# An fp32 decoder trunk on one core: one plain block instead of two at the start of three channel mixers

## The chip, the cores and the metric

The kernel runs on one core of a Trainium2 chip, as one launch. Its time is the device time of an execution in microseconds, given as the median of several runs. A core has five engines with queues of their own: PE (matrix products, with the weight loads shown apart as PEld), DVE (vector work), ACT (activations and copies), POOL (general work) and SP, which here only issues transfers (DMAs). SBUF is the memory that the engines work from, PSUM holds the matrix products in eight banks, and DRAM is outside the core.

## The reference

A trunk of two layers works on `x` of 512 tokens by 1024 channels in float32, and ends in an RMSNorm. Each layer has two channel mixers around a token mixer: latent attention (MLA) in layer 0, sparse attention (NSA) in layer 1.

```python
def rmsnorm(x, g):
    y = x * lax.rsqrt(jnp.mean(x * x, axis=-1, keepdims=True) + RMS_EPS)
    return y * g

def swiglu(x, w_gate, w_up, w_down):
    return (jax.nn.silu(x @ w_gate) * (x @ w_up)) @ w_down

for i in range(2):
    h = h + 0.5 * swiglu(rmsnorm(h, ffn_norm_a[i]), ffn_a_w_gate[i], ffn_a_w_up[i], ffn_a_w_down[i])
    h = h + mixer_i(rmsnorm(h, mix_norm[i]))        # MLA, then NSA
    h = h + 0.5 * swiglu(rmsnorm(h, ffn_norm_b[i]), ffn_b_w_gate[i], ffn_b_w_up[i], ffn_b_w_down[i])
return rmsnorm(h, final_norm)
```

The change touches the channel mixers alone. There are four of them, called a0, b0, a1 and b1 in order of time, with `idx` 0 to 3. `w_gate` and `w_up` are 1024 x 2816, `w_down` is 2816 x 1024.

## The kernel before

**Layout.** The residual is kept transposed: eight tiles `h` (channels c, 128 partitions, 512 tokens in the free dimension). A product of weights and activations is made in three matrix products, since each operand is split into a rounded high part and the remainder: high by high, high by low, low by high. A split (`split`, L173 to L181) is one ACT copy that rounds (L177) and one DVE subtraction that leaves the low part (L178). The norm's gain is a factor in the split of `h`; the factor 1/rms of a token is one row of 512 numbers, which is multiplied in behind the matrix products.

**A channel mixer** (`ffn`, L416) runs over 22 hidden blocks of 128 hidden columns, f = 0 to 21. A block yields the gate and the up projection, each 128 hidden columns by 512 tokens, in one of two forms:

- A *plain* block (`plain`, L404): for the gate and the up slab, 8 channel chunks, 2 halves of the tokens and 3 products, 96 matmuls of 128x256.
- A *sums* block (`wsums`, L328, and `product`, L371): the 2 x 2 product of (gate, up weights, by halves of the channels) and (activations, by halves of channels and tokens) in seven products instead of eight, each of 4 chunks x 3, 84 matmuls of 128x256. The seven products are run in the order 1, 7, 6, 2, 5, 4, 3 (L532 to L545). Products 1, 2 and 3 use raw quarters of the activations; products 7, 6, 5 and 4 use sums of quarters. Of the weights, products 1 and 2 use the gate slab's halves, 4 the second half of the up slab, and 7, 6, 3 and 5 use sums of halves, which DVE adds (L359, L360, L363, L364) and ACT and DVE split.

`PLAIN = 3, 2, 2, 2` (L50) is the number of plain blocks at the start of each mixer. While these run, the sums of the activations are made (`combine`, L231, once for each pair p = 0 to 3 of chunks p and p + 4): ACT scales two `h` tiles into `y` (L240), DVE makes four quarters' sums in `u` (L244 to L246), and ACT and DVE split `u` into a tile `four` (L177, L178). Tiles `y` and `u` are taken from the rotating tags `fh` and `fl`, three buffers each, which also hold the split weights of the sums blocks.

**The plain blocks' weights** of mixers 1 to 3 are not split there. They are finished during the mixer before: at its blocks 12 to 20 `make_load` fetches a quarter slab, `make` splits it, and POOL writes the high and the low half to DRAM (L396); at the mixer's start `made_slab` (L398) loads 1 MiB, both parts of a slab, into one of three weight tiles (L401).

**The norm's row** of mixers 1 to 3 comes out of the first plain block's squares: PE sums them over partitions (L269), POOL takes the power, DVE transposes (L292), and POOL sends the result through DRAM, spread to all partitions (L293, L295, tile `row<-nrow`). The gates of the plain blocks (`gate`, L425: DVE times the row, ACT's Silu, DVE times the row) wait for it.

**From the sums blocks on** a block's matrix products end in ACT's copies: product 1 from bank `px` to `pg` (L533), 7 and 6 to the tile `uq` (L535, L537; one buffer), 5 to `pg` (L540). Two DVE additions finish the up half (L542, L544). Behind each block stand pieces of the down projection (`unit`, L460), the products of 128x512 of L169 to L171, from the third or so block on.

**What sets the order.** Every engine works its queue in order. The queue's order follows the program, with what is ready earlier by the scheduler's model ahead of what is late; `high_priority` puts a few instructions ahead, and `issue_after` puts instructions behind a given one on their engine. So the weight instructions of the second sums block stand behind the copies of the first (`after(copies, i)` in `wsums`, L357 to L368).

Of the kernel before, what the change touches and what calls it, by code (L numbers as in the profile page):

```python
# [49 lines left out]
PLAIN = 3, 2, 2, 2  # L50
# [3 lines left out]
READY = 12  # L54
# [11 lines left out]
class Kern:  # L66
# [13 lines left out]
    def setup(self):  # L80
# [4 lines left out]
        self.nw, self.odd, self.nq, self.made, self.quarter = 0, 0, 0, {}, {}  # L85
# [145 lines left out]
    def combine(self, p):  # L231


        nc, fp = self.nc, self.fp
        y = fp.tile([P, 1024], F32, tag="fh", bufs=3, name="y")
        u = fp.tile([P, 1024 + 2 * PAD], F32, tag="fl", bufs=3, name="u")[:, :1024]
        for e in range(2):
            c = p + KP * e
            with self.tc.issue_after(self.weights.ins) if self.weights else nullcontext():
                nc.scalar.activation(y[:, e * S : e * S + S], self.h[c], AF.Copy, scale=self.gains[:, self.ng + c : self.ng + c + 1])  # L240
            self.weights = None
        q = lambda t, i: t[:, i * HS : i * HS + HS]
        two = lambda t: t.rearrange("p (a n) -> p a n", n=HS)
        nc.vector.tensor_tensor(two(u[:, :S]), q(y, 1)[:, None, :].to_broadcast([P, 2, HS]), two(y)[:, 0:4:3, :], op=ALU.subtract)  # L244
# [19 lines left out]
    def norm_col(self, n, s2, urgent=0, eps=None, col=None):  # L264

        nc = self.nc
        pc = self.bank("o", "pc")
# [60 lines left out]
    def wsums(self, idx, f, copies=None):  # L328


        nc, fp, w_gu = self.nc, self.fp, self.a["w_gu"]
        rg = fp.tile([P, 1024], F32, tag="fr", bufs=3, name="rg")
# [27 lines left out]
        nc.vector.tensor_tensor(u0, u0, g0, op=ALU.add)  # L360
# [10 lines left out]
    def product(self, j, w, out, first, last):  # L371
        mm = self.nc.tensor.matmul
        wh, wl = w[j]
        for p in range(KP):
# [5 lines left out]
    def made_tile(self, idx, f, z):  # L380
        if (idx, f, z) not in self.made:
            self.made[idx, f, z] = self.dp.tile([P, 2048], F32, name=f"made{idx}{f}{z}")[:, :]
        return self.made[idx, f, z]

    def make_load(self, idx, i):
        self.raw = self.sp.tile([P, S], F32, tag="s2", bufs=2, name="wm")
        with self.tc.issue_after(self.gate_load.ins):
            self.nc.sync.dma_start(self.raw, self.a["w_gu"][idx, i // 4, i // 2 % 2][:, i % 2 * S : i % 2 * S + S])

    def make(self, idx, i):  # L390

        hi, lo = [self.quarter[2 * (i % 2) + x] for x in range(2)]
        self.split(self.raw, hi, lo)
        d = self.made_tile(idx, i // 4, i // 2 % 2).rearrange("p (z e n) -> p z e n", z=2, e=2)
        for z, t in enumerate((hi, lo)):
            self.nc.gpsimd.dma_start(d[:, z, i % 2, :], f32v(t))  # L396

    def made_slab(self, idx, f, z):  # L398
        wh, wl = self.wtiles("half")
        both = bass.AP(tensor=wh.tensor, offset=wh.offset, ap=[list(wh.ap[0]), [wl.offset - wh.offset, 2], [1, 1024]])  # L400
        self.nc.sync.dma_start(f32v(both), self.made[idx, f, z].rearrange("p (z n) -> p z n", z=2))  # L401
        return [t.rearrange("p (k c) -> p k c", c=P) for t in (wh, wl)]

    def plain(self, idx, f, z, out):  # L404

        wh, wl = self.ahead.pop(0) if self.ahead else self.made_slab(idx, f, z) if idx else self.wslab(self.a["w_gu"][idx, f, z], (KC, P), "half")
# [9 lines left out]
    def ffn(self, idx, gain_next, ap, tp):  # L416
# [8 lines left out]
        def gate(f, g):  # L425

            t = tg[f] = tp.tile([P, S], F32, tag="tg", bufs=2, name="tg")
            nc.vector.tensor_tensor(t, g, row, op=ALU.mult)
# [58 lines left out]
        def plain_acts():  # L487
            for e, g in enumerate(gates):
                gate(e, g)
# [4 lines left out]
        for f, g in enumerate(gates):  # L494
            u = tu[f] = self.bank(("mm", "S")[f % 2], "pu")
            self.plain(idx, f, 0, g)
            if f == 0 and idx:
# [3 lines left out]
                self.norm_col(D, self.s2, URGENT, col=row[:, 0:P:32])  # L501
# [12 lines left out]
            for p in (((0, 1), (2, 3)) if plain == 2 else ((0, 1), (2,), (3,)))[f]:  # L514
                self.combine(p)

        tail, left = (NF - 2) // NG * NG, 1
        for f in range(plain, NF):
# [6 lines left out]
            w = self.wsums(idx, f, copies if idx and f == plain + 1 else None)  # L525
            if f == plain:
# [7 lines left out]
            self.product(7, w, q, True, False)  # L534
# [3 lines left out]
            self.product(2, w, g[:, :HS], False, True)  # L538
# [7 lines left out]
            if f == plain and idx:  # L546
                with self.after(copies, 3):
# [944 lines left out]
```

## Time and profile before

| What | us |
| --- | --- |
| Median of 3 runs | 1856.54 (1856.47 to 1857.44) |
| The profiled execution, its own time | 1855.04 |
| Its span (first to last instruction) | 1853.3 |
| Busy in the span: PE, DVE, ACT, POOL | 1834.6, 1529.1, 1090.8, 275.9 |
| First matmul of a0, b0, a1, b1 | 5.9, 543.2, 877.7, 1507.2 |

The granted clock of PE is full throughout, and the transfers average 117 GB/s. The profile is of one execution, so its durations and its span belong together, and a sum is made against the span; the execution's own time is 1.7 us above it, and the median is 1.5 us above that. A matmul's duration in the trace overlaps the next one's, so its pace is read from starts. MLA lies between the mixers a0 and b0, NSA between a1 and b1; a1 follows b0 directly.

### The profile page before, as it was taken

What the parts mean: (1) busy time and instruction counts of PE and PEld (TensorE: products, weight loads), DVE (VectorE), ACT (ScalarE), POOL (GpSimd) and SP (SyncE); (2) the same over time, 40 slices, a digit from 0 to 9 for tenths busy, and PEclk for the clock granted to TensorE, in tenths of its full rate; (3) what the DMA queues carried; (4) which work ended last, traced back from release to release, by engine and by line L of the source; (5) the groups of instructions that cost most, each with busy time, mean ns of one, the idle gap of its engine ahead of it and who ended that gap; (6) DMA issues with size and microseconds to landing.
All of it is one profiled execution on the core that took longest, in us unless ns stands there. A gap on an engine that the chain in (4) does not pass through costs nothing.

```text
span 1853.3 us, 32953 instructions
## 1 busy us (share of the span) xinstructions
PE 1834.6 (99%) x12392; PEld 1674.9 (90%) x12392; DVE 1529.1 (83%) x2785; ACT 1090.8 (59%) x2033; POOL 275.9 (15%) x398
## 2 busy tenths in 40 slices
PE   8999999999999999999999999999999999999998
PEld 8999999888889999998999999988888889999997
DVE  7988886578779888876998888755988979888885
ACT  7555554579766555544655555426977856555554
POOL 0000000156510000000000000015665500000000
PEclk9999999999999999999999999999999999999999
DMA  7334433142352345433333443233222143333321
GB/s 259 118 120 154 154 124 105 56 110 72 95 176 99 105 143 166 160 115 122 110 115 130 161 160 99 91 106 108 75 86 74 47 163 121 108 107 103 103 90 57
DMA packets 88047, 216.31 MB, mean 117 GB/s; under 512 B 11176, under 2 KB 39232, under 8 KB 87888
## 3 DMA queue, kind: packets, MB, share of 16 engines
q1 hardware_dynamic: 80272, 195.01, 33.2%
q0 software_dynamic: 4512, 14.17, 2.0%
q10 hardware_dynamic: 3104, 5.03, 0.8%
q8 instruction: 97, 1.59, 0.4%
q14 instruction: 62, 0.51, 0.1%
HBM read 192.33 MB, written 14.76 MB: 112 GB/s over the span
## 4 chain that ended last, share of the span: by engine, by line
PE 87%; DVE 7%; ACT 2%; issue 1%; DMA 1%; POOL 1%; SPq 0%; DVEq 0%; ACTq 0%; POOLq 0%
PE pd L169 8%; PE pd L171 8%; PE pd L170 8%; PE px L376 5%; PE px L377 5%; PE px L378 5%; PE pg L376 4%; PE pg L378 4%; PE pg L377 4%; PE pq L376 4%; PE pq L377 4%; PE pq L378 4%; PE o L1295 2%; PE pt L1270 2%; PE po L169 2%; PE po L171 2%
## 5 line engine op out<-in xcount | busy, mean ns | idle before, releaser
L170 PE MATMUL pd<-al,wd 128*128 128x512 f32 x576 | 224.1, 389 | 0.0
L171 PE MATMUL pd<-ah,wd 128*128 128x512 f32 x576 | 224.0, 389 | 0.0
L169 PE MATMUL pd<-ah,wd 128*128 128x512 f32 x576 | 224.0, 389 | 0.0
L376 PE MATMUL px<-four,wh 128*128 128x256 f32 x632 | 175.3, 277 | 2.8 <-ACT uq L537 1.4
L178 DVE TENSOR_TENSOR w<-rg,w 128x1024 fp32r<-128x1024 f32 x79 | 96.3, 1222 | 96.4 <-ACT w L177 96.4
L376 PE MATMUL pq<-four,wh 128*128 128x256 f32 x632 | 174.5, 276 | 0.4 <-DVE tu L439 0.4
L378 PE MATMUL px<-four,wl 128*128 128x256 f32 x632 | 174.7, 276 | 0.0
L377 PE MATMUL px<-four,wh 128*128 128x256 f32 x632 | 174.5, 276 | 0.0
L377 PE MATMUL pq<-four,wh 128*128 128x256 f32 x632 | 174.5, 276 | 0.0
L378 PE MATMUL pq<-four,wl 128*128 128x256 f32 x632 | 174.5, 276 | 0.0
L458 DVE SCALAR_TENSOR_TENSOR h<-pd,h 128x512 f32<-128x512 f32 x216 | 147.0, 681 | 6.1 <-PE pd L171 6.1
L177 ACT ACTIVATE wd<-wdr 128x384 fp32r<-128x384 f32 x192 | 98.5, 515 | 67.9 <-PE pd L170 38.3
L171 PEld LDWEIGHTS pd<-ah,wd 128*128 128x128 f32 x576 | 108.2, 188 | 22.5
L169 PEld LDWEIGHTS pd<-ah,wd 128*128 128x128 f32 x576 | 108.1, 188 | 19.3
L170 PEld LDWEIGHTS pd<-al,wd 128*128 128x128 f32 x576 | 108.1, 188 | 19.4
L376 PEld LDWEIGHTS px<-four,wh 128*128 128x128 f32 x632 | 118.6, 188 | 4.1 <-ACT uq L537 2.1
L177 ACT ACTIVATE w<-rg 128x1024 fp32r<-128x1024 f32 x79 | 83.8, 1060 | 61.9 <-PE pg L378 56.6
L376 PEld LDWEIGHTS pq<-four,wh 128*128 128x128 f32 x632 | 118.6, 188 | 0.5 <-ACT w L177 0.5
L378 PEld LDWEIGHTS px<-four,wl 128*128 128x128 f32 x632 | 118.6, 188 | 0.4 <-DVE wl L178 0.2
L396 POOL DMA_DIRECT2D made<-x x48 | 26.0, 542 | 622.9 <-ACT pg L533 404.5
L377 PEld LDWEIGHTS px<-four,wh 128*128 128x128 f32 x632 | 118.6, 188 | 0.0
L378 PEld LDWEIGHTS pq<-four,wl 128*128 128x128 f32 x632 | 118.6, 188 | 0.0
(368 smaller groups left out, 6059.6 us busy)
## 6 DMA issues: line engine op xcount, KB each, us to landing
wr<-in_w_gu SPq DMA_DIRECT2D x81, 512.0 KB, 4.1
rg<-in_w_gu SPq DMA_DIRECT2D x79, 512.0 KB, 3.4
wdr<-in_w_down SPq DMA_DIRECT2D x192, 192.0 KB, 2.4
made<-x POOLq DMA_DIRECT2D x48, 256.0 KB, 2.8
w<-made SPq DMA_DIRECT2D x12, 1024.0 KB, 5.3
wm<-in_w_gu SPq DMA_DIRECT2D x24, 256.0 KB, 3.9
wdr<-in_w_down SPq DMA_DIRECT2D x24, 256.0 KB, 2.7
wr<-in_mla_w_o SPq DMA_DIRECT2D x8, 512.0 KB, 3.6
```

The lines of the kernel that those rows point to most:

```text
L169: mm(out, wh, xh, start=first, stop=False)
L170: mm(out, wh, xl, start=False, stop=False)
L171: return mm(out, wl, xh, start=False, stop=last)
L177: nc.scalar.activation(hi, src, AF.Copy)
L178: (nc.gpsimd if pool else nc.vector).tensor_tensor(lo, src, f32v(hi), op=ALU.subtract)
L376: mm(out, wh[:, p], xh, start=first and p == 0, stop=False, skip_group_check=True)
L377: mm(out, wh[:, p], xl, start=False, stop=False, skip_group_check=True)
L378: mm(out, wl[:, p], xh, start=False, stop=last and p == KP - 1, skip_group_check=True)
L396: self.nc.gpsimd.dma_start(d[:, z, i % 2, :], f32v(t))
L458: nc.vector.scalar_tensor_tensor(self.h[c], p, 0.5, self.h[c], op0=ALU.mult, op1=ALU.add)
L1270: nc.tensor.transpose(pt[:, j * P : j * P + P], p_sb[:, j * P : j * P + P], self.ident)
L1295: mm(out, vs[g][:, j, br * P : (br + 1) * P], x, start=False, stop=last and t == 1 and j == 2 * z + 1, skip_group_check=True)
```

## The change

The last three mixers get one plain block instead of two (`PLAIN = 3, 1, 1, 1`). What was their second plain block, f = 1, is now a sums block. To make that possible:

1. *Its weights are finished in DRAM.* The weights of block 1 are kept there in their final, split form: gate slab (products 1 and 2), up and its sum (7 and 4), the two full sums (6 and 3) and the half sum (5). Three and a half MiB with the plain block's two slabs. `made_sums` loads them into the tiles that `wsums` would have filled. Instead of eight splits during the mixer before there are eleven, at its blocks 9 to 20 (`READY = 9`).
2. *The sums of these weights are made by transfers.* At blocks 5 to 8 of the mixer before (`FIRST`), `make_sum` has POOL copy a half slab from the weights to a DRAM buffer, and a second transfer adds another half slab, or an earlier sum, to it. Ahead of the copy POOL runs a one-element copy that reads `uq`, the `mark`.
3. *The input's sums* (`combine`) take `y` from the tag of the raw up slabs (`wr`, two buffers) and `u` from that of the raw gate slabs (`fr`, three), so that `fh` and `fl` are free for block 1's weights.
4. *In block 1* the last quarter of product 7, which reads the fourth pair's sums, comes behind the first half of product 2.
5. *The weights of block 2* (`wsums(idx, f + 1, copies)`) are put ahead of the plain block's gate, which is queued behind `self.summed`, one of the weights' additions. `pu` of the plain block and the norm's column sum change PSUM banks (`o` and `mm`).

```diff
-PLAIN = 3, 2, 2, 2
+PLAIN = 3, 1, 1, 1
-READY = 12
+FIRST = 5
+READY = 9
...
     def combine(self, p):
-        y = fp.tile([P, 1024], F32, tag="fh", bufs=3, name="y")
-        u = fp.tile([P, 1024 + 2 * PAD], F32, tag="fl", bufs=3, name="u")[:, :1024]
+        if self.ng == GAINS["a0"]:
...
+        else:
+            y = self.wp.tile([P, 1024], F32, tag="wr", bufs=2, name="y")
+            u = fp.tile([P, 1024], F32, tag="fr", bufs=3, name="u")
...
     def wsums(self, idx, f, copies=None):
+        if (idx, f, "g") in self.made:
+            return self.made_sums(idx, f)
...
-        nc.vector.tensor_tensor(u0, u0, g0, op=ALU.add)
+        self.summed = nc.vector.tensor_tensor(u0, u0, g0, op=ALU.add)
...
+    def make_split(self, t, at, d):
+        hl = [self.quarter[2 * at + z] for z in range(2)]
+        self.split(t, *hl)
+        for z in range(2):
+            self.nc.gpsimd.dma_start(d[:, z], f32v(hl[z]))
+
+    def make_sum(self, idx, f, z):
+        g, w = self.nc.gpsimd, self.a["w_gu"]
+        half = lambda x, e: w[idx, f, x][:, e * S : e * S + S]
+        pre = self.pre.setdefault(idx, [])
+        first, add = ((half(1, 0), half(1, 1)), (half(1, 0), half(0, 0)), (half(0, 0), pre and pre[0]), (half(0, 1), pre and pre[-1]))[z]
+        pre.append(self.dp.tile([P, S], F32, name=f"ws{z}{f}{idx}")[:, :])
+        g.dma_start(pre[z], first)
+        g.dma_start(pre[z], add, accum_op=ALU.add, max_dma_last_dim=4 * S)
+
+    def make_steps(self, idx):
...
+        parts = [(half(0, z, e), to(0, z)[:, :, e]) for z in range(2) for e in range(2)]
+        parts += [(half(f, 0, e), to(f, "g")[:, :, e]) for e in range(2)]
+        parts += [(half(f, 1, 1), to(f, "u")[:, :, 1]), (pre[1], to(f, "u")[:, :, 0]),
+                  (pre[0], to(f, "s")[:, 0, :]), (pre[2], to(f, "h")[:, :, 0]), (pre[3], to(f, "h")[:, :, 1])]
...
+    def made_sums(self, idx, f):
...
+        use(1, 2, *self.made_slab(idx, f, "g"))
+        for name, i, j in (("u", 7, 4), ("h", 6, 3)):
+            hl = self.sum_tiles(1024)
+            for z in range(2):
+                nc.sync.dma_start(f32v(hl[z]), self.made[idx, f, name][:, z * 1024 : z * 1024 + 1024])
+            use(i, j, *hl)
...
     def ffn(self, idx, gain_next, ap, tp):
...
-            u = tu[f] = self.bank(("mm", "S")[f % 2], "pu")
+            u = tu[f] = self.bank("o" if idx else ("mm", "S")[f % 2], "pu")
...
-            w = self.wsums(idx, f, copies if idx and f == plain + 1 else None)
-            if f == plain:
+            w = ready.pop() if ready else self.wsums(idx, f)
+            if f == plain and idx == 0:
                 plain_acts()
...
-            self.product(7, w, q, True, False)
+            self.product(7, w, q, True, False, range(KP - (f == 1)))
+            if f == 1:
+                self.product(2, w, g[:, :HS], False, False, range(2))
+                self.product(7, w, q, False, False, range(KP - 1, KP))
...
             if f == plain and idx:
+                ready.append(self.wsums(idx, f + 1, copies))
+                plain_acts(self.summed)
...
-                i = f - READY
-                if 0 < i <= 4 * PLAIN[idx + 1]:
-                    self.make(idx + 1, i - 1)
-                if 0 <= i < 4 * PLAIN[idx + 1]:
-                    self.make_load(idx + 1, i)
+                if FIRST <= f < FIRST + 4:
+                    mark = nc.gpsimd.tensor_copy(self.gains[:, 63:64], uq[:, HS : HS + 1])
+                    with self.tc.issue_after(mark.ins):
+                        self.make_sum(idx + 1, PLAIN[idx + 1], f - FIRST)
+                if f == READY:
+                    make = self.make_steps(idx + 1)
+                if f >= READY and make:
+                    for step in make.pop(0):
+                        step()
```

Lines of the changed kernel have other numbers: L249 to L251 are the sums of `combine` (L244 to L246 before), L179 the low part of a split (L178), L366, L367 and L370 three of the weights' additions (L359, L360 and L363), L383 to L385 the products (L376 to L378), L481 the gate's first multiplication (L428), L402 the writes of finished weights (L396).

How the change moves instructions is seen at three places. First DVE at the start of the second mixer, b0. Before, the sums of the third and fourth pair (`u`, from `y`) stand among the weight instructions (`s1`, `ru`, `w`, `wl`) of the first sums block:

```order
L178 TENSOR_TENSOR four_6579<-u_6573,four_6579 128x1024
L245 TENSOR_TENSOR u_6583<-y_6582,u_6583 128x256
L360 TENSOR_TENSOR ru_6594<-ru_6594,rg_6592 128x512
L246 TENSOR_TENSOR u_6583<-y_6582,u_6583 128x256
L178 TENSOR_TENSOR w_6597<-rg_6592,w_6597 128x1024
L178 TENSOR_TENSOR wl_6603<-ru_6594,wh_6602 128x1024
L178 TENSOR_TENSOR four_6589<-u_6583,four_6589 128x1024
```

Now, with the weights of the second sums block behind them, and then the gate of the plain block (`tg`):

```order
L249 TENSOR_TENSOR u_6517<-y_6516 128x512
L251 TENSOR_TENSOR u_6507<-y_6506,u_6507 128x256
L250 TENSOR_TENSOR u_6517<-y_6516,u_6517 128x256
L251 TENSOR_TENSOR u_6517<-y_6516,u_6517 128x256
L179 TENSOR_TENSOR four_6513<-u_6507,four_6513 128x1024
L179 TENSOR_TENSOR four_6523<-u_6517,four_6523 128x1024
L179 TENSOR_TENSOR w_6640<-rg_6635,w_6640 128x1024
L366 TENSOR_TENSOR s1_6639<-wr_6637 128x512
L367 TENSOR_TENSOR wr_6637<-wr_6637,rg_6635 128x512
L481 TENSOR_TENSOR tg_6659<-pg_6367,row_6365 128x512
```

The weight instructions that stood between the last two low parts (`four`) are behind them now, and belong to the next block.

On PE, in the first sums block of b0 after the change, `pq` takes product 7 and `pg` product 2; `four_6513` and `four_6523` are the third and the fourth pair:

```order
L383 MATMUL pq_6541<-four_6513,wh_6528 128x256
L384 MATMUL pq_6541<-four_6513,wh_6528 128x256
L385 MATMUL pq_6541<-four_6513,wl_6529 128x256
L383 MATMUL pg_6542<-x_6220,w_6526 128x256
L384 MATMUL pg_6542<-x_6220,w_6526 128x256
L385 MATMUL pg_6542<-x_6220,w_6526 128x256
L383 MATMUL pg_6542<-x_6265,w_6526 128x256
L384 MATMUL pg_6542<-x_6265,w_6526 128x256
L385 MATMUL pg_6542<-x_6265,w_6526 128x256
L383 MATMUL pq_6541<-four_6523,wh_6528 128x256
L384 MATMUL pq_6541<-four_6523,wh_6528 128x256
L385 MATMUL pq_6541<-four_6523,wl_6529 128x256
```

Six matmuls of product 2 stand ahead of the three that read the fourth pair; in a sums block of before all of product 7 came first.

On POOL, from the middle of a0 on, before the change there were only the writes of finished weights:

```order
L295 DMA row_158<-nrow_395 128x512
L396 DMA made100_2478<-x_100 128x512
L396 DMA made100_2478<-x_110 128x512
L396 DMA made100_2478<-x_114 128x512
L396 DMA made100_2478<-x_118 128x512
L396 DMA made101_2832<-x_100 128x512
```

Now, with the mark (`gains<-uq`), the copy (L411) and the adding transfer (L412) of each sum:

```order
L300 DMA row_158<-nrow_395 128x512
L615 COPY gains_77<-uq_941 128x1
L411 DMA ws011_1077<-in_w_gu 128x512
L412 DMA ws011_1077<-in_w_gu 128x512
L402 DMA made1_0_0_1791<-x_100 128x512
L615 COPY gains_77<-uq_1107 128x1
L411 DMA ws111_1260<-in_w_gu 128x512
L402 DMA made1_0_0_1791<-x_110 128x512
L412 DMA ws111_1260<-in_w_gu 128x512
L402 DMA made1_0_0_1791<-x_114 128x512
```

The writes of finished weights now stand between the sums' transfers, in one queue with the marks.

More of the change, by code (lines that the diff above doesn't have):

```diff
@@ L369, in wsums, with product @@
         return w
-    def product(self, j, w, out, first, last):
+    def product(self, j, w, out, first, last, ps=range(KP)):
         mm = self.nc.tensor.matmul
         wh, wl = w[j]
-        for p in range(KP):
+        for p in ps:
             xh, xl = self.xc[j, p]
@@ L390, in make, with made_tile @@
[L390 to L398, printed above, removed]
+    def made_tile(self, *key):
+        if key not in self.made:
+            self.made[key] = self.dp.tile([P, 2048], F32, name="made" + "_".join(map(str, key)))[:, :]
+        return self.made[key]
@@ L399, in made_slab, with use @@
+    def made_slab(self, *key):
         wh, wl = self.wtiles("half")
         both = bass.AP(tensor=wh.tensor, offset=wh.offset, ap=[list(wh.ap[0]), [wl.offset - wh.offset, 2], [1, 1024]])
-        self.nc.sync.dma_start(f32v(both), self.made[idx, f, z].rearrange("p (z n) -> p z n", z=2))
-        return [t.rearrange("p (k c) -> p k c", c=P) for t in (wh, wl)]
+        self.nc.sync.dma_start(f32v(both), self.made[key].rearrange("p (z n) -> p z n", z=2))
+        return wh, wl
+    def made_sums(self, idx, f):
+        nc, fp, w = self.nc, self.fp, {}
+        def use(i, j, hi, lo):
+            for n, k in enumerate((i, j) if j else (i,)):
+                w[k] = [t[:, n * S : n * S + S].rearrange("p (k c) -> p k c", c=P) for t in (hi, lo)]
+        use(1, 2, *self.made_slab(idx, f, "g"))
[4 more added lines that the diff above has]
+            use(i, j, *hl)
+        hi = fp.tile([P, S], F32R, tag="sh", bufs=2, name="wh")
+        lo = fp.tile([P, S + 2 * PAD], F32R, tag="sl", bufs=2, name="wl")[:, 2 * PAD :]
+        for z, t in enumerate((hi, lo)):
+            nc.sync.dma_start(f32v(t), self.made[idx, f, "s"][:, z * S : z * S + S])
+        use(5, None, hi, lo)
+        return w
@@ L404, in plain @@
     def plain(self, idx, f, z, out):
-        wh, wl = self.ahead.pop(0) if self.ahead else self.made_slab(idx, f, z) if idx else self.wslab(self.a["w_gu"][idx, f, z], (KC, P), "half")
+        wh, wl = self.ahead.pop(0) if self.ahead else [t.rearrange("p (k c) -> p k c", c=P) for t in self.made_slab(idx, f, z)] if idx else self.wslab(self.a["w_gu"][idx, f, z], (KC, P), "half")
         mm = self.nc.tensor.matmul
@@ L423, in ffn, with gate @@
         tg, tu, units = {}, {}, []
-        def gate(f, g):
+        def gate(f, g, behind=None):
             t = tg[f] = tp.tile([P, S], F32, tag="tg", bufs=2, name="tg")
-            nc.vector.tensor_tensor(t, g, row, op=ALU.mult)
+            with self.tc.issue_after(behind.ins) if behind else nullcontext():
+                nc.vector.tensor_tensor(t, g, row, op=ALU.mult)
             nc.scalar.activation(t, t, AF.Silu, scale=-1.0)
@@ L484, in ffn, with plain_acts @@
                 tokens(t)
-        def plain_acts():
+        def plain_acts(behind=None):
             for e, g in enumerate(gates):
-                gate(e, g)
+                gate(e, g, behind)
                 act(e)
@@ L500, in ffn @@
                         self.sumsq(self.h[c])
-                self.norm_col(D, self.s2, URGENT, col=row[:, 0:P:32])
+                self.norm_col(D, self.s2, URGENT, col=row[:, 0:P:32], tag="mm")
                 self.norm_row(row, URGENT)
@@ L513, in ffn @@
                 self.norm_row(row)
-            for p in (((0, 1), (2, 3)) if plain == 2 else ((0, 1), (2,), (3,)))[f]:
+            for p in {1: ((0, 1, 2, 3),), 2: ((0, 1), (2, 3)), 3: ((0, 1), (2,), (3,))}[plain][f]:
                 self.combine(p)
-        tail, left = (NF - 2) // NG * NG, 1
+        ready = []
+        tail, left = (NF - 2) // NG * NG, NG - plain or 1
         for f in range(plain, NF):
@@ L537, in ffn @@
             copies.append(nc.scalar.activation(uq[:, HS:], x, AF.Copy))
-            self.product(2, w, g[:, :HS], False, True)
+            self.product(2, w, g[:, :HS], False, True, range(2 * (f == 1), KP))
             self.product(5, w, x, False, True)
```

27 lines of the change are left out of this document (17 added, 10 removed).

## The prediction

> **What bounds the kernel now.** I read the page's busy times and its chain first, then PE's own waits, then the stretches around the three starts that the change rewrites.
>
> ```profile
> span 1853.3 us, 32953 instructions
> ...
> PE 87%; DVE 7%; ACT 2%; issue 1%; DMA 1%; POOL 1%; SPq 0%; DVEq 0%; ACTq 0%; POOLq 0%
> ```
>
> ```profile
> PE pg L412 <- ACT w L150: 5.9, 1, 5.9
> PE px L376 <- ACT uq L537: 1.4, 2, 0.7
> PE px L376 <- ACT pg L533: 1.3, 2, 1.0
> ```
>
> PE carries the end, and inside a channel mixer it hardly ever waits: after the kernel's first 5.9 us, the whole trace has 2.7 us of waits on ACT's copies at L533 and L537. So a matmul taken out is worth its pace, unless its absence uncovers something else. The windows show where that could be:
>
> ```profile
> 543.20:554.60 11.40, 11.40 (x101) 11.38 (x100) 9.75 (x19) 8.32 (x13) 1.72 (x2) 1.00 0.86 314
> 554.60:565.40 10.80, 10.80 (x98) 10.80 (x97) 10.80 (x15) 6.54 (x7) 0.58 (x1) 1.00 0.23 84
> 565.40:575.00 9.60, 9.60 (x87) 9.60 (x86) 9.45 (x13) 8.39 (x15) 0.00 (x0) 1.00 0.20 66
> 575.00:580.00 5.00, 3.96 (x35) 3.77 (x34) 5.00 (x10) 2.04 (x4) 0.00 (x0) 1.00 0.23 88
> ...
> 915.00:920.00 5.00, 4.31 (x35) 3.92 (x34) 5.00 (x8) 4.24 (x8) 0.00 (x0) 1.00 0.10 39
> 1545.00:1550.00 5.00, 4.31 (x35) 3.92 (x34) 5.00 (x9) 4.32 (x8) 0.00 (x0) 1.00 0.08 21
> ```
>
> The columns are PE, PEld, DVE, ACT and POOL busy, then the granted clock (1.00 throughout), DMA share and GB/s. Two plain blocks and two sums blocks follow 543.2. DVE is full from 554.6 on and idle for 1.65 us before; PE loses 1.04 us at 579 and 0.69 at each of the two later starts. These stretches hold PE and DVE both at their limit: that is where the result is decided.
>
> **The matmuls.** The pace comes from starts, since the duration of one (276 ns) overlaps the next:
>
> ```profile
> 543.22 0.28 PE L412 MATMUL pg<-x,w 128*128 128x256 f32 x1
> ...
> 565.94 0.28 PE L376 MATMUL px<-x,w 128*128 128x256 f32 x1
> ...
> 575.46 0.28 PE L376 MATMUL px<-x,w 128*128 128x256 f32 x1
> ...
> 578.07 0.28 PE L378 MATMUL pq<-four,wl 128*128 128x256 f32 x1
> 579.38 0.39 PE L376 MATMUL px<-four,wh 128*128 128x256 f32 x1 [1.04 <-ACT pg L533]
> ```
>
> Between 565.94 and 575.46 lie the 84 matmuls of one sums block: 9.52 us, or 0.1133 each. A plain block has 2 x 8 x 2 x 3 = 96, so 10.88 us; two of them and the norm's small matmuls fill 543.22 to 565.94 (22.72 = 21.76 + 0.96). One plain block becomes a sums block in three mixers: 3 x 12 x 0.1133 = **4.08 us** less.
>
> The Trainium skill ("TensorE: Matmul & The Clock Gate", Back-to-back issue gap) puts a sustained stream of weight load and matmul at about 81 ns for 128 columns and 131 for 512. Halfway by columns that is an estimate of 98 ns for 256, and 36 of them would be worth 3.5 us. The trace does not agree (113 ns for 256 columns here), so the row decides.
>
> **The input's sums.** All four pairs must now be ready after one plain block. This is how DVE makes the last ones before:
>
> ```profile
> 546.17 0.68 DVE L244 TENSOR_TENSOR u<-y 128x512 f32<-128x512 f32 x1
> ...
> 554.85 0.68 DVE L359 TENSOR_TENSOR s<-ru 128x512 f32<-128x512 f32 x1
> ...
> 556.94 0.69 DVE L360 TENSOR_TENSOR ru<-ru,rg 128x512 f32<-128x512 f32 x1
> ...
> 557.87 1.22 DVE L178 TENSOR_TENSOR w<-rg,w 128x1024 fp32r<-128x1024 f32 x1
> 559.01 1.22 DVE L178 TENSOR_TENSOR wl<-ru,wh 128x1024 fp32r<-128x1024 f32 x1
> 560.14 1.22 DVE L178 TENSOR_TENSOR four<-u,four 128x1024 fp32r<-128x1024 f32 x1
> 561.28 0.68 DVE L363 TENSOR_TENSOR rg<-rg,s 128x512 f32<-128x512 f32 x1
> ```
>
> By starts, 512 columns take 0.60 us of DVE and 1024 take 1.14. The first sum starts at 546.17 and the last low part is done at 561.28. Four weight instructions stand among them (0.60 + 0.60 + 1.14 + 1.14 = 3.5 us); they leave this place, since the first sums block's weights come finished from DRAM. So 557.8 at the latest. The new order also lets the first two pairs' y be scaled before the last chunks, some 1 us earlier, but then ACT and DVE take turns (copy, sum, high part, low part): walking the new order with these durations I get 557.5. The block starts at 543.22 + 10.88 + 0.96 = 555.06, and the fourth pair is first read after product 1 (12), three quarters of product 7 (9) and half of product 2 (6): 27 x 0.1133 = 3.06 us, so 558.1. It fits by half a microsecond: cost nothing, with a bound of 561.28 - 558.1 = 3.2 us at each start if the sums keep their old pace.
>
> **The weights from DRAM.**
>
> ```profile
> 543.41 0.52 SPq L401 DMA_DIRECT2D w<-made  x1
> ...
> 545.00:550.00 5.00, 5.00 (x47) 5.00 (x46) 4.50 (x10) 5.00 (x8) 0.00 (x0) 1.00 0.96 370
> 550.00:555.00 5.00, 5.00 (x46) 5.00 (x46) 4.08 (x8) 2.32 (x4) 1.72 (x2) 1.00 0.97 351
> ```
>
> The third slab goes out at 543.41, when its tile comes free, and then the queue runs at 350 to 370 GB/s. After the change that third slab is product 1's, and the rest follows: 3.5 MiB in all, at 360 GB/s 10.2 us, so 553.7, before the first of it is needed at 555.06. Hidden. The second sums block's weights wait for y's tile: y of the third pair is read by 554, and a load takes 4.1 us,
>
> ```profile
> wr<-in_w_gu SPq DMA_DIRECT2D x81, 512.0 KB, 4.1
> ```
>
> so 558 against a first use on DVE at 559: hidden by a microsecond, and DVE pays if not.
>
> **What is left for DVE and ACT.** Over these blocks DVE has the same weight sums as before and 0.67 us more by starts (the two adds of 256 columns, L542 and L544, for the block that is no longer plain, at about 0.34 each as half of 0.60 and a little more), in 1.36 us less of PE time. New as well: the gate of the plain block is reached by DVE at 560.1 in the new order, and needs the norm's row, which went through DRAM:
>
> ```profile
> 551.11 0.31 DVE L292 STREAM_TRANSPOSE row<-row 128x128 f32<-128x128 f32 x1 [0.93 <-POOL row L284]
> ...
> 556.90 0.58 POOL L295 DMA_DIRECT2D row<-nrow  x1 [4.42 <-issue]
> ```
>
> ```profile
> row<-nrow POOLq DMA_DIRECT2D x6, 256.0 KB, 3.7
> ```
>
> Before, 556.90 + 3.7 = 560.6 was early for the gate at 563.1. Now the transpose comes 0.7 us later behind a low part, so the row lands near 561.2 and DVE stands for about 1 us. At the start at 877.7 that trip is 2 us shorter and nothing waits. What is late next is told by the stall of before:
>
> ```profile
> 578.42 0.63 ACT L429 ACTIVATE tg<-tg 128x512 f32<-128x512 f32 x1 [2.59 <-DVE tg L428]
> 578.96 0.37 ACT L533 ACTIVATE pg<-px 128x256 f32<-128x256 f32 x1
> ```
>
> ACT stood 2.59 us at a Silu that waited for DVE, and the copy that PE needed was queued behind it. In the new order the same copies stand behind other instructions that wait for DVE: the split of the third block's first weights holds product 6, the next block's first high part holds the copy before product 5. My walk gives 0.8 us of PE standing at 543, 0.6 at 878, 1.2 at 1507, together 2.6 against the 2.4 of before. Bounds: all three gone (-2.4), or all of the lost cover on top (3 x (1.36 + 0.67) = +6.1). I take **-0.2**: near no change, as the stretches have the same owner, with somewhat more work in its queue before them.
>
> **The making.** Three mixers split 11 halves instead of 8.
>
> ```profile
> L178 DVE TENSOR_TENSOR x<-wm,x 128x512 fp32r<-128x512 f32 x24 | 16.4, 682 | 0.0
> L177 ACT ACTIVATE x<-wm 128x512 fp32r<-128x512 f32 x24 | 15.1, 630 | 6.5 <-DMA wm<-in_w_gu 6.2
> ```
>
> ```profile
> 700.00:750.00 50.00, 50.00 (x371) 47.20 (x370) 42.86 (x68) 27.25 (x47) 3.79 (x7) 1.00 0.50 160
> ```
>
> Nine more of 0.68 us on DVE and 0.63 on ACT, one to a block. A block with its share of the down projections takes some 15 us (9.52 and 24 matmuls of twice the pace), and DVE is idle for 14% of a stretch in the middle of a mixer: 2 us to spare; the 24 of before cost PE at most one wait. +0.1. The 24 new transfers go through POOL:
>
> ```profile
> DMA to landing us min/median/max: 2.6/2.9/6.5
> ```
>
> ```profile
> 581.84 0.36 ACT L537 ACTIVATE uq<-px 128x256 f32<-128x256 f32 x1
> 596.21 0.36 ACT L535 ACTIVATE uq<-pq 128x256 f32<-128x256 f32 x1
> ```
>
> The row on landing is of the 256 KB writes to DRAM. An adding transfer between two places in DRAM has no row. POOL stands between the copy and the add, and its mark reads uq, a single tile, which ACT writes again 14 us later (581.84 to 596.21): POOL has that long. Nearest row 2.9 us, twice that for the add at most: hidden, zero; from below nothing, from above rival three.
>
> **Sum:** 1853.3 - 4.08 - 0.2 + 0.1 = 1849.1 us of span. The profiled execution took 1855.04, 1.5 below the median 1856.54, so by difference: 1856.54 - 4.2 = **1852.3**.
>
> **Rivals.**
> 1. *The starts clear up* (18%). The weights' 3.5 us leave DVE just where it fell behind, and the three stalls go: -4.08 - 2.4 gives 1850.1. For: 1.65 us of DVE idle to use. Against: DVE is full for 45 us after.
> 2. *DVE gives it all back* (18%). Its work is the same, so the end of the stretch is where DVE is done: PE stalls grow by up to 2.03 us at each start, 1856.54 - 4.08 + 6.1 = 1858.6, likelier half of that, 1855.5. For: 5.00 of 5.00 in every window where PE waits. Against: PE gets ahead of it again with the down projections.
> 3. *The input's sums are late* (7%). If they end at 561.28 as before, product 7 stands 3.2 us, three times: +9.5 - 4.08, 1861.9. It eats the gain from 1.36 us late (559.5) and makes the kernel slower by over 0.2% from 2.6 late. Against: the 3.5 us that leave. The same end by POOL (3%): if copy and add take over 14 us, ACT's copy waits in twelve blocks, each microsecond over costing 12.
>
> **How the numbers follow.** The forecast has 54%. What a measurement can tell from no change is about 0.2%, 3.7 us, so faster means below 1852.8, which cuts my likeliest case: within its 1850.8 to 1853.8 about two thirds lie below. Faster: 0.18 + 0.36 = 0.54; same: 0.18 + 0.18 = 0.36; slower: 0.10. The range takes in rival one and the likelier half of rival two: 1849.4 to 1856.6.
>
> **What would show it.** The sums block that replaces a plain one should start 11.8 us after the mixer and run its 84 matmuls in 9.5 us; a PE wait at product 7 on the low part of the fourth sum is rival three, waits of over 3 us in all on ACT's copies in the second and third sums block are rival two. DVE should wait for the row at the starts at 543 and 1507. No PE wait may appear at blocks 5 to 9; one there, behind ACT's uq, is POOL's chain. I am wrong in kind if PE waits at the starts grow beyond 6 us together, or if PE's count of matmuls is not 36 less.

## The result and the profile after

The changed kernel takes 1875.96 us (median of 4 runs, 1872.98 to 1879.47) against 1856.54 before: a ratio of 1.0104, 95% interval 1.0085 to 1.0123. It is slower by 19.4 us; 1852.3 was forecast. The profiled execution took 1874.61 us with a span of 1872.8, 19.5 above that of before.

PE has 36 matmuls fewer, as counted (12392 to 12356), and yet the span grew. The first lines of the page, and PE's longest waits in the channel mixers behind the kernel's first load:

```profile
span 1872.8 us, 33045 instructions
...
PE 1839.0 (98%) x12356; PEld 1675.7 (89%) x12356; DVE 1538.2 (82%) x2800; ACT 1101.2 (59%) x2054; POOL 312.8 (17%) x452
```

```profile
PE px L383 <- ACT pg L587: 7.0, 6, 1.8
PE pg L383 <- ACT pg L597: 5.2, 3, 2.5
PE pq L385 <- DVE wl L179: 4.0, 2, 2.2
PE px L383 <- ACT uq L594: 1.1, 1, 1.1
```

The columns of the waits are the total, the count and the longest. L587 is the copy of product 1, L597 that of product 5, L179 the low part of a split. These waits make 17.3 us, against 2.7 before. A second loss shows in the granted clock. Windows of the changed kernel, with the same columns as in the prediction (granted clock, DMA share and GB/s last):

```profile
560.00:565.00 5.00, 5.00 (x45) 5.00 (x44) 3.06 (x4) 1.40 (x3) 0.60 (x1) 1.00 0.88 306
565.00:570.00 5.00, 3.58 (x31) 3.38 (x30) 1.39 (x3) 4.77 (x7) 0.00 (x0) 1.00 0.31 102
570.00:575.00 5.00, 2.72 (x18) 2.23 (x17) 5.00 (x8) 2.39 (x4) 0.00 (x0) 0.88 0.22 62
575.00:580.00 5.00, 5.00 (x32) 4.79 (x33) 5.00 (x9) 2.57 (x6) 0.00 (x0) 0.78 0.42 147
...
908.00:911.00 3.00, 0.52 (x5) 0.49 (x5) 1.97 (x4) 1.87 (x4) 0.00 (x0) 1.00 0.55 193
911.00:914.00 3.00, 3.00 (x20) 3.00 (x19) 2.86 (x5) 1.91 (x3) 0.00 (x0) 0.62 0.16 61
914.00:917.00 3.00, 3.00 (x23) 3.00 (x23) 2.63 (x4) 1.77 (x4) 0.00 (x0) 0.81 0.54 175
```

After the waits at 572.89 and 910.51 the clock is down: by 0.12 and 0.22 of 5 us and by 0.38 and 0.19 of 3 us, which is worth 3.4 us in all. Taking every matmul of the channel mixers from the trace, and the distance of its start from the one before against its pace (0.1133 us for 256 columns, twice that for 512), the loss is 36.44 us against 13.17 before. That is 23.3 more; less the 4.1 of the matmuls that are gone it gives 19.2 of the 19.5.

**The starts.** The prediction saw DVE at its limit here. At first DVE is far from it: it is busy for 1.39 of 5 us from 565, because it waits for the norm's row (timeline of POOL and DVE, then the row's line of the transfers issued between 543 and 575):

```profile
560.32 0.60 POOL L300 DMA_DIRECT2D row<-nrow  x1 [4.18 <-issue]
568.61 0.69 DVE L481 TENSOR_TENSOR tg<-pg,row 128x512 f32<-128x512 f32 x1 [5.39 <-DMA row<-nrow]
```

```profile
row<-nrow POOLq DMA_DIRECT2D x1, 256.0 KB, 8.3
```

The row is issued at 560.32 and lands 8.3 us later, where the prediction took 3.7 (6.9 and 7.0 at the two later starts). Just ahead of it SP had issued the loads of the third sums block (559.43 and 559.81), and with it the first one of the fourth (560.57). The first of these is late as well, and on ACT a copy that PE waits for stands behind its split:

```profile
559.43 0.33 SPq L340 DMA_DIRECT2D rg<-in_w_gu  x1
559.81 0.42 SPq L346 DMA_DIRECT2D wr<-in_w_gu  x1
560.57 0.33 SPq L340 DMA_DIRECT2D rg<-in_w_gu  x1
...
565.09 1.06 ACT L178 ACTIVATE w<-rg 128x1024 fp32r<-128x1024 f32 x1 [2.14 <-DMA rg<-in_w_gu]
566.05 1.04 ACT L178 ACTIVATE wh<-wr 128x1024 fp32r<-128x1024 f32 x1
567.00 0.36 ACT L597 ACTIVATE pg<-px 128x256 f32<-128x256 f32 x1
```

PE stands before 567.41 for that copy (product 5's, at 567.00) and before 572.89 for a low part of DVE, which has 5.4 us of standing to catch up and is busy without a break from 570 on.

**The middle of the mixers.** Five waits of 0.7 to 1.9 us, 7.2 us together, stand where the next mixer's weights are made (in blocks 6, 8 and 9), all of one kind. A sixth, 1.2 us at 621, is of another: there a split of down weights waits for its load. The first of the five, from the timelines of POOL, SP, ACT and PE:

```profile
128.65 0.86 POOL L412 DMA_DIRECT2D ws<-ws  x1 [3.32 <-issue]
130.78 0.43 SPq L395 DMA_DIRECT2D wm<-in_w_gu  x1
136.65 0.63 ACT L178 ACTIVATE x<-wm 128x512 fp32r<-128x512 f32 x1 [2.07 <-DMA wm<-in_w_gu]
137.19 0.37 ACT L587 ACTIVATE pg<-px 128x256 f32<-128x256 f32 x1
137.61 0.38 PE L383 MATMUL px<-four,wh 128*128 128x256 f32 x1 [1.70 <-ACT pg L587]
```

The adding transfer (L412) runs, the load of a half slab (`wm`) issued 2.1 us later takes 5.8, its split stands on ACT ahead of product 1's copy, and PE waits for the copy. The load's line of the transfers between 127 and 138, and the landing of all such loads in the kernel before:

```profile
wm<-in_w_gu SPq DMA_DIRECT2D x1, 256.0 KB, 5.8
```

```profile
DMA to landing us min/median/max: 3.4/3.9/4.6
```

While the adding transfer runs, the DMA engines are nearly as busy as with plain loads, at less than half the rate; the changed kernel, then the kernel before at the same place:

```profile
130.00:131.50 1.50, 1.50 (x9) 1.23 (x8) 1.50 (x3) 0.62 (x2) 0.00 (x0) 1.00 0.79 126
```

```profile
131.00:133.00 2.00, 2.00 (x11) 1.65 (x11) 2.00 (x3) 0.91 (x2) 0.00 (x0) 1.00 0.85 298
```

### The profile page after: what moved, and what is told of

It reads as the page before. It is cut to its first block, busy times and chain, and to the rows that moved or that the text cites. A ratio compares the mean times of both kernels' runs of the same rounds, so it can differ in the third digit from the quotient of the medians.

```text
span 1872.8 us, 33045 instructions
## 1 busy us (share of the span) xinstructions
PE 1839.0 (98%) x12356; PEld 1675.7 (89%) x12356; DVE 1538.2 (82%) x2800; ACT 1101.2 (59%) x2054; POOL 312.8 (17%) x452
## 5 line engine op out<-in xcount | busy, mean ns | idle before, releaser
L383 PE MATMUL px<-four,wh 128*128 128x256 f32 x656 | 183.5, 280 | 8.3 <-ACT pg L587 7.0
L385 PE MATMUL pq<-four,wl 128*128 128x256 f32 x656 | 181.5, 277 | 4.0 <-DVE wl L179 4.0
L383 PE MATMUL pq<-four,wh 128*128 128x256 f32 x656 | 181.4, 277 | 0.4 <-DVE tu L492 0.4
L384 PE MATMUL px<-four,wh 128*128 128x256 f32 x656 | 181.5, 277 | 0.0
L384 PE MATMUL pq<-four,wh 128*128 128x256 f32 x656 | 181.4, 277 | 0.0
L385 PE MATMUL px<-four,wl 128*128 128x256 f32 x656 | 181.4, 276 | 0.0
L179 DVE TENSOR_TENSOR w<-rg,w 128x1024 fp32r<-128x1024 f32 x79 | 96.7, 1223 | 89.0 <-ACT w L178 88.8
L178 ACT ACTIVATE wd<-wdr 128x384 fp32r<-128x384 f32 x192 | 98.6, 516 | 67.2 <-PE pd L171 30.1
L383 PEld LDWEIGHTS px<-four,wh 128*128 128x128 f32 x656 | 123.2, 188 | 11.3 <-ACT pg L587 8.6
L385 PEld LDWEIGHTS pq<-four,wl 128*128 128x128 f32 x656 | 123.3, 188 | 4.3 <-DVE wl L179 4.3
L383 PEld LDWEIGHTS pq<-four,wh 128*128 128x128 f32 x656 | 123.3, 188 | 0.6 <-ACT w L178 0.6
L385 PEld LDWEIGHTS px<-four,wl 128*128 128x128 f32 x656 | 123.2, 188 | 0.4 <-DVE wl L179 0.4
L384 PEld LDWEIGHTS pq<-four,wh 128*128 128x128 f32 x656 | 123.4, 188 | 0.0
L384 PEld LDWEIGHTS px<-four,wh 128*128 128x128 f32 x656 | 123.3, 188 | 0.1
L178 ACT ACTIVATE w<-rg 128x1024 fp32r<-128x1024 f32 x79 | 83.8, 1061 | 64.7 <-PE pg L385 53.9
```

Source lines behind the costliest of these rows:

```text
L178: nc.scalar.activation(hi, src, AF.Copy)
L179: (nc.gpsimd if pool else nc.vector).tensor_tensor(lo, src, f32v(hi), op=ALU.subtract)
L383: mm(out, wh[:, p], xh, start=first and p == 0, stop=False, skip_group_check=True)
L384: mm(out, wh[:, p], xl, start=False, stop=False, skip_group_check=True)
L385: mm(out, wl[:, p], xh, start=False, stop=last and p == KP - 1, skip_group_check=True)
```

## The experiments

Two causes are to be told apart from each other and from the prediction's own rivals. Theory A: transfers are late, at the starts because the row shares the DMA engines with the weights, in the middle because of the adding transfers. Theory B: the order and load of DVE and ACT, whatever the transfers do. The median of the kernel before beside these runs was 1856.54 to 1856.83.

| Kernel | median us | ratio to before, 95% interval |
| --- | --- | --- |
| the change | 1875.96 | 1.0104 (1.0085 to 1.0123) |
| row not spread through DRAM | 1869.21 | 1.0068 (1.0053 to 1.0083) |
| no sums by transfers | 1866.67 | 1.0057 (1.0039 to 1.0076) |
| no adding transfers | 1868.70 | 1.0065 (1.0050 to 1.0080) |
| making behind the block's copies | 1875.19 | 1.0095 (1.0080 to 1.0110) |
| sums on DVE | 1866.96 | 1.0052 (1.0035 to 1.0070) |
| one split of block 3 later | 1879.25 | 1.0120 (1.0096 to 1.0144) |
| splits of blocks 3 to 6 later | 1879.52 | 1.0112 (1.0095 to 1.0129) |
| the same, and loads held for the row | 1868.49 | 1.0067 (1.0051 to 1.0083) |
| sums on DVE and loads held | 1858.98 | 1.0011 (1.0002 to 1.0021) |
| the same, down weights' splits later | 1855.01 | 0.9989 (0.9980 to 0.9998) |
| the kernel before, with the adding transfers | 1860.52 | 1.0016 (1.0005 to 1.0027) |

**The row's trip taken away.**

```diff
-        nc.gpsimd.dma_start(row, bass.AP(tensor=d.tensor, offset=d.offset, ap=[[0, P], [1, S]]))
+        if not urgent:
+            nc.gpsimd.dma_start(row, bass.AP(tensor=d.tensor, offset=d.offset, ap=[[0, P], [1, S]]))
...
-        self.nc.gpsimd.memset(row[:, 0:P], 0.0)
+        self.nc.gpsimd.memset(row, 0.0)
```

> Leaves out: in the last three mixers the norm's row is not spread through DRAM; the gates multiply by a tile that is ready at once, so the norm's factor is missing there. Everything else is the changed kernel. Theory A (the transfers are late: the row lands 8.3 us after its issue instead of 3.7, because it shares the DMA engines with the loads of the second and third sums block): DVE's waits of 5.39 us at 568.6 and 3.68 at 1546.1 vanish, with them PE's waits of 2.39 and 1.89 us on a low part at 572.9 and 1550.4 and the lower clock (0.88 and 0.78) from 570 to 580: 4.3 + about 2 us, near 1870. Theory B (DVE has too much to do there, whatever the row does): PE's waits only move to the next copies, and less than 2 us is won: above 1874.

1869.21, 6.8 less. The waits on the low part at the second and fourth mixer (2.39 and 1.89) are gone, with the first of them the clock's drop at 574; what is left at the starts are the waits on product 5's copy (1.39, 0.56 and 1.82). That is theory A: with DVE relieved of one wait, no other took its place at the starts.

**The sums' transfers taken away**, both, and the adding one alone.

```diff
-        pre.append(self.dp.tile([P, S], F32, name=f"ws{z}{f}{idx}")[:, :])
-        g.dma_start(pre[z], first)
-        g.dma_start(pre[z], add, accum_op=ALU.add, max_dma_last_dim=4 * S)
+        pre.append(first)
```

> Leaves out: the sums of the weights by transfers (copy and adding transfer); the finished weights of block 1 are made from raw halves instead, loaded as the others are. So the up half of block 1 is wrong by its weights, with the same number of instructions on PE, DVE and ACT. Theory A (the adding transfers fill the DMA engines at 60 to 150 GB/s, so the loads behind them land 5 to 6 us after issue instead of 4, and the split of such a load stands on ACT ahead of the copy that PE waits for): PE's waits of 1.86 us at 137.6, 1.40 at 678.6, 1.93 at 973, 0.72 at 1005 and 1.34 at 1020 vanish: 7.2 us less, near 1869. Theory B (the split stands ahead of the copy and waits for its load in any case): two thirds or more of these waits stay, above 1873.

```diff
-        g.dma_start(pre[z], add, accum_op=ALU.add, max_dma_last_dim=4 * S)
```

> Leaves out: the adding transfer alone; the copy into the DRAM buffer stays. So the sums of the weights of block 1 lack one summand. Theory A in its narrow form (it is the adding that fills the DMA engines): the same five waits of 7.2 us vanish, near 1869, as without both transfers. If the copy does as much as the adding, about half stays: 1872.

1866.67 and 1868.70: 9.3 less without both, 7.3 without the adding. The waits after 137, 678, 973, 1005 and 1020 are gone in both (one of 1.0 us at 125 is left in the first). Without the adding transfer the load that took 5.8 us takes 4.0 at the same place. The gain is not these five waits alone: the wait at 621 grew by 1 us in both profiles, and of the two drops of the clock at the starts the first kernel shows none and the second one. Most of the cost is the adding; whether the copies cost the other 2 us can't be told, since the two intervals overlap.

**The making moved on ACT**, the transfers kept.

```diff
-                    for step in make.pop(0):
-                        step()
+                    with self.tc.issue_after(copied.ins):
+                        for step in make.pop(0):
+                            step()
```

> Computes the reference. The step of the making that belongs to a block (its load and its split) is queued behind that block's last copy of product 5 on ACT, in place of three blocks earlier and just ahead of the copy of product 1. If the order on ACT turns a late load into PE's wait, the five waits in the middle of the mixers vanish though the transfers stay: 7.2 us less, near 1869. If the split or its writes are wanted earlier than that, or if the adding transfers slow what PE needs in another way, it stays above 1873, and a new wait shows at the end of the mixers.

1875.19: no gain to be told from the spread. PE's waits between the starts, those over 0.2 us counted, fell from 8.8 to 4.7 us, but its profiled execution had 1.2 and 2.6 us of waits at 31.8 and 46.5, in the first mixer, ahead of anything that this edit touches. So this run does not settle how much of the cost is the order on ACT.

**The sums on DVE.** The halves are loaded into two tiles in turn, and DVE adds one to the other in place; marks, copies and adding transfers go, and the making begins one block earlier.

```diff
-        g.dma_start(pre[z], add, accum_op=ALU.add, max_dma_last_dim=4 * S)
...
+        def add():
+            self.nc.vector.tensor_tensor(got["A"], got["A"], got["B"], op=ALU.add)
...
+        return [[L(0, p[0][0])], [C(0, p[0][1]), L(1, p[1][0])], [C(1, p[1][1]), L(2, p[2][0])], [C(2, p[2][1]), L(3, p[3][0])],
+                [C(3, p[3][1]), L("A", u0)], [L("B", g0)],
+                [C("B", to(f, "g")[:, :, 0]), add, L("B", u1, False)],
...
```

> Computes the reference. The sums of block 1's weights are made by DVE on the loaded halves (four additions of 512 columns per mixer, 0.60 us each, 7.2 us in all), and the copies, the adding transfers and POOL's marks are gone; ten loads per mixer for eleven splits. If the transfers were the cost, it is as fast as the kernel without them (1866.7), since DVE has 2 us to spare in each block: 1864 to 1869. If what was won there came from something else that leaving them out changed (fewer marks, raw halves), or if DVE's additions cost PE their 7.2 us, it is 1872 or more.

1866.96, the time of the kernel without the transfers. So the transfers are what costs. Twelve additions of 512 columns on DVE cost nothing that is seen; they lie in the middle of the mixers, where DVE has room.

**The order at the starts alone**, in two forms: the first split of block 3 behind block 1's copy of product 5, and those of blocks 3 to 6 each behind the block before's copy of product 1.

```diff
-            w = ready.pop() if ready else self.wsums(idx, f)
+            with self.tc.issue_after(early.ins) if idx and f == plain + 2 else nullcontext():
+                w = ready.pop() if ready else self.wsums(idx, f)
...
+            if f == plain:
+                early = copied
```

> Computes the reference. In the last three mixers the first split of the third sums block's weights is queued on ACT behind the first sums block's copy of product 5, in place of ahead of it. If that split, which waits for a load, is what makes PE wait at 567.4, 910.5 and 1545.4 (1.59, 2.64, 1.45 us), 5 us go and the lower clock at 911 to 917 with them: near 1869. If the row that is late sets the pace of these blocks, the waits move to the next copies: above 1874.

```diff
+            with self.tc.issue_after(copies[0].ins) if idx and plain + 2 <= f < plain + 6 else nullcontext():
+                w = ready.pop() if ready else self.wsums(idx, f)
```

> Computes the reference. The changed kernel with the first splits of blocks 3 to 6 behind the block before's copy of product 1, as in the kernel with held loads (1868.49), but the loads are not held. If it is the row's earlier landing that won 7.5 us there, this one stays near the changed kernel, 1874 or above, and DVE waits 3 us and more for the row at the second and fourth mixer's start. If the order on ACT won it, 1868.

1879.25 and 1879.52: no gain, rather a loss of 3 us (their lowest runs, 1873.77 and 1875.92, lie among those of the change). The gain of 5 us that was expected did not come. PE's waits on product 5's copy shrink from 5.2 to 1.4 and 0.6 us, and PE comes sooner to the low part that DVE is late with, because it waits for the row. Waits of PE and of DVE in the second form:

```profile
PE pq L385 <- DVE wl L179: 6.9, 2, 3.7
```

```profile
DVE tg L481 <- DMA row<-nrow: 12.6, 3, 6.6
```

**The loads held until the row has landed**, with the second form of the order. A small transfer on SP that reads the row stands ahead of the third sums block's loads.

```diff
-        nc.sync.dma_start(ru, w_gu[idx, f, 1])
+        last = nc.sync.dma_start(ru, w_gu[idx, f, 1])
+        if idx and f == PLAIN[idx] + 1:
+            with self.tc.issue_after(last.ins):
+                self.held = nc.sync.dma_start(self.dp.tile([1, 64], F32, name="hold")[:, :], self.row[0:1, 2 * P : 2 * P + 64])
...
-        self.gate_load = nc.sync.dma_start(rg, w_gu[idx, f, 0])
+        with self.tc.issue_after(self.held.ins) if idx and f == PLAIN[idx] + 2 else nullcontext():
+            self.gate_load = nc.sync.dma_start(rg, w_gu[idx, f, 0])
...
```

> Computes the reference. In the last three mixers the loads from the third sums block on are held until the norm's row has landed (a 256-byte transfer on SP that reads the row stands ahead of them), and the first splits of blocks 3 to 6 are queued behind the block before's copy of product 1. Theory A (the row and the weights share the DMA engines): the row lands 4 to 5 us after its issue instead of 8.3, DVE's wait for it falls from 5.39 to about 1 us, PE's 11.3 us of waits at the three starts fall to some 4 and the clock stays at 1.00: near 1865. Theory B (DVE has too much to do): the row comes early and PE waits as long: above 1872.

1868.49: 7.5 less than the change, 11.0 less than the same order without the hold, and between the two expectations. The row's landing at the second mixer, and DVE's wait for it over all mixers:

```profile
row<-nrow POOLq DMA_DIRECT2D x1, 256.0 KB, 3.3
```

```profile
DVE tg L485 <- DMA row<-nrow: 0.4, 1, 0.4
```

3.3 us instead of 8.3 (9.5 with the order alone), and 0.4 us of waiting instead of 10.0. Holding back the prefetches by some microseconds makes the row, and what waits for it, earlier. It also makes one load late: at the last start PE now waits 2.7 us before 1543.03, behind a split of down weights, and the clock drops after it. That is the wait that the last but one experiment below removes. The Trainium skill ("DMA: Bandwidth & Descriptors", Issuing engines are not separate DMA queues) says that transfers issued by different engines run on the same 16 DMA engines and interleave; these rows agree, for the row goes out on POOL's queue and lands in 3.3 us or in 9.5, as SP's loads are held or not.

**Both together.** The edits of the sums on DVE and of the held loads in one kernel.

> Computes the reference. The sums on DVE and the held loads together. If the two costs are separate and add up, 9 us from the one and 11 from the other: 1876 - 20 = 1856, about the time of the kernel before. If the lower clock and the same DVE queue make them one cost, less than 14 is won: above 1862.

1858.98, 17.0 less than the change: 9.0 and 7.5 add up. Against the expected 1856 it is 3 us more, and the profile shows where. In the last mixer (timelines of ACT and PE, and a window):

```profile
1533.55 0.52 ACT L178 ACTIVATE wd<-wdr 128x384 fp32r<-128x384 f32 x1 [3.22 <-DMA wdr<-in_w_down]
1533.98 1.04 ACT L178 ACTIVATE wh<-rg 128x1024 fp32r<-128x1024 f32 x1
1534.93 0.36 ACT L602 ACTIVATE pg<-px 128x256 f32<-128x256 f32 x1
...
1535.35 0.39 PE L387 MATMUL px<-four,wh 128*128 128x256 f32 x1 [2.90 <-ACT pg L602]
```

```profile
1535.00:1540.00 5.00, 4.41 (x23) 4.20 (x24) 4.95 (x7) 3.50 (x9) 0.00 (x0) 0.66 0.49 173
```

A split of the first down weights (`wd`), whose load is late behind the held ones, stands ahead of product 1's copy.

**That split behind the copy.**

```diff
-                work(tag, copied if tag == "S" else None)
+                work(tag, copied if tag == "S" else copies[0] if idx and f < plain + 4 else None)
```

> Computes the reference. As the kernel with the sums on DVE and the held loads (1858.98), and the splits of the first down weights are queued behind the block's copy of product 1 in the last three mixers. In the kernel without this PE waits 3.06 us at 1535.3 for a copy that stands on ACT behind such a split, whose load lands 5.1 us after its issue, and the clock is 0.66 for the next 5 us (1.7 us). Theory (order on ACT turns a late load into PE's wait): these 4.8 us go, 1854.2, two to three below the kernel before. If the late load only meets the next instruction, it stays at 1857 or above.

1855.01 (11 runs, 1854.43 to 1856.54), 4.0 less, with no drop of the clock until the last 2 us of the span. So one plain block in three mixers can be faster than two, by little: 0.9989 of the kernel before, interval 0.9980 to 0.9998, that is 0.4 to 3.7 us.

**The transfers in the kernel before.** Marks, copies and adding transfers as in the change, at its blocks 5 to 8, with nothing that reads the sums.

```diff
+                if 5 <= f < 9:
+                    mark = nc.gpsimd.tensor_copy(self.gains[:, 63:64], uq[:, HS : HS + 1])
+                    with self.tc.issue_after(mark.ins):
+                        self.make_sum(idx + 1, PLAIN[idx + 1], f - 5)
```

> Computes the reference. The kernel before, with the marks, copies and adding transfers of the change put in at the same blocks; nothing reads their sums. If these transfers slow a mixer by themselves, it takes 6 to 9 us more than the kernel before, 1863 to 1866. If they only hurt together with the making that the change moved to the same time (a split waiting for its load ahead of PE's copy), less than 2 us: below 1859.

1860.52, 3.8 more (0.9 to 5.0): between the two expectations. The making of before begins as the last adding transfer of each mixer runs, so they meet once per mixer; there PE waits, 1.02, 1.40 and 1.62 us, 4.0 in all. One of the three:

```profile
664.17 0.84 POOL L388 DMA_DIRECT2D ws<-ws  x1 [3.18 <-issue]
666.49 0.43 SPq L398 DMA_DIRECT2D wm<-in_w_gu  x1
671.90 0.63 ACT L177 ACTIVATE x<-wm 128x512 fp32r<-128x512 f32 x1 [1.62 <-DMA wm<-in_w_gu]
```

At the three earlier adding transfers of each mixer, where no such load follows, PE does not wait. So the transfers hurt by the load that they delay, and the change has moved more such loads behind them.

## Why the prediction was wrong

- **The matmuls** (4.08 us): the count was right. In the last kernel above 1.7 us of it are left.
- **The input's sums**: right. The fourth pair's low part ends at 560.54, and PE, whose first sums block starts at 557.50 (11.85 us after the mixer, 11.8 forecast), needs it 3.06 us later, at 560.56. PE does not wait there, but there is no margin, where half a microsecond was forecast; that it fits is in part luck. Rival three's first form did not come.
- **The norm's row** failed: "Now the transpose comes 0.7 us later behind a low part, so the row lands near 561.2 and DVE stands for about 1 us". That DVE would wait for the row was right. The failed term is the landing: its price of 3.7 us was that of the row before, when the DMA share of its window was 0.23; now it is 0.88 (560 to 565). The row landed after 8.3, and DVE stood for 5.4 us and 3.7 at two starts and 0.9 at the third, where nothing was to wait.
- **The weights from DRAM** failed in "Hidden": the sum took the first sums block's 3.5 MiB (block 1's alone; with the plain block's two slabs the finished weights of a mixer are 5.5 MiB) and the second block's loads, and these came in time. The third block's loads, the first of the fourth and the row are issued in the same 15 us, and whether these delay each other was not asked.
- **The starts' stalls**, "I take -0.2", with 6.1 as the bound: PE waits at the three starts rose by about 9 us (by the starts of matmuls, 11.7 against 2.9, waits over 0.2 us counted), and the clock took 3.4 more. That is the "beyond 6 us together" by which the prediction was to be wrong in kind. The owner of the waits was not the amount of DVE's work, on which rivals one and two both turn, but transfers that were late. Neither rival came: the note that over 3 us of waits on ACT's copies would be rival two would have misled, for DVE stood idle at the same time.
- **The making**, "+0.1", and the adding transfer, "hidden, zero": 9.0 to 9.3 us by the kernels without these transfers. The landing time was bounded well (4.3 us, against 2.9 to 5.8), and POOL's marks were in time, so rival three's second form did not come either. What was left out is the resource: the transfer holds the DMA engines, and a load behind it lands late in front of a copy that PE needs. The prediction said that no PE wait may appear at blocks 5 to 9; the five waits stand at blocks 6, 8 and 9, behind product 1's copy and not behind `uq`.
- **The clock** was taken as 1.00. It fell to 0.50 after two of PE's longer waits.

What stays open: how much of the adding transfers' cost an order on ACT could save (the run on it drowned in the first mixer's spread). Of the 4.1 us, 2.4 are missing in the last kernel. In its profiled execution the matmuls of the channel mixers lose 4.5 us more by their starts than before, 1.1 of them in the first mixer; what causes these small losses was not followed up.

## What to carry to other kernels

A landing time is a price at a load: before it is used elsewhere, add up all bytes that are issued in the same window, by every queue, and look at what DMA share the old row was read at. When a small transfer that everybody waits for shares a window with prefetches, hold the prefetches; and on an in-order engine keep a split that waits for a load behind the copies that the matrix engine waits for, since a model of the schedule places it by a landing time that may not hold. Such an edit does not pay while another transfer is late: one won 4.0 us once the row was early, two others won nothing before. Twelve additions on an engine with room cost nothing that could be seen, while the same additions by transfers, meant to be free, cost 9 us.

## What was not expected of the hardware

- **The clock falls after short waits.** In the profiles of these kernels 18 waits of PE in the channel mixers were 2.1 us or longer (by starts). After all nine of 2.59 us and more, and after four of the nine between 2.1 and 2.4, the granted clock went to 0.50. It stayed there for 3.4 us after ten of these waits, and for 6.8 after the three of 3.3 us and more: windows of 1.5 us from 910.5 on in the changed kernel show 0.91, 0.50, 0.50 and 0.95, so 1.7 us of work are lost on top of the wait. After waits below 2.1 us it fell only where another wait lay within 5 us ahead, and this twice: behind 1.8 and 1.7 us with the sums on DVE, and behind 1.7 us and during 1.4 with the first form of the order. Other such pairs passed without a drop (1.45 and 1.89 us at 1545 and 1550 in the changed kernel). The Trainium skill ("TensorE: Matmul & The Clock Gate", Part 1: The HAM clock gate) puts the drop after an idle window of about 3.4 us that runs freely; the length of the slow stretch agrees with it (3.41 us, or twice that), and the wait that suffices is shorter here (2.1 us for a single one).
- **An adding transfer between two places in DRAM** of 256 KB lands after 3.8 to 4.9 us, beside 2.8 to 4.3 for a plain copy, and holds the DMA engines at a share of 0.79 for 126 GB/s in the windows shown, where plain loads had 298 GB/s at 0.85.
- **The first mixer's start varies.** PE's wait near 43 to 47 us, ahead of what any of these edits reaches, was 0.3 to 2.6 us in the profiles of these kernels.
